# Hybrid decoder block, down projection: GpSimd's additions given to VectorE, the final norm's squares put into another buffer, the last two row blocks normed by halves

## The chip, the core and the metric

The kernel runs on one core of one Trainium2 chip. The metric is the device time of one execution in microseconds (us); a kernel's time is the median of its runs.

## The reference, cut to what matters

The block mixes tokens (an S5 state space branch and an RWKV-7 branch), projects, and ends with a squared-ReLU MLP and a final RMSNorm. Only the last product and the norm are touched here: `hid` has 2048 tokens of 4096 features, `w_down` is 4096 by 1024, `h` is 2048 by 1024, all in float32.

```python
hn = rms_norm(h, norm_ffn_g[i])
h = h + jnp.square(jax.nn.relu(hn @ w_up[i])) @ w_down[i]
return rms_norm(h, norm_final_g)
```

## The kernel before, in words

The program's last stage is `mlp_down`. It computes `hid @ w_down` by a Strassen scheme (Winograd's form): a block of 2 by 2 sub-blocks is multiplied with seven products in place of eight. The products are numbered 1 to 7 and stand in the order 1, 5, 6, 2, 7, 3, 4 (`ORDER`).

The 4096 features are cut into eight groups (`gr`), 512 features each. Within a group eight steps (`c`) go over the tokens; a step adds to two row blocks of 128 tokens, `r0` and `r1`, which stay in SBUF for the whole stage as `acc0` to `acc15` (`r0` of step c is `acc(2c)`, `r1` is `acc(2c+1)`). Their halves of 512 columns are `a11`, `a12` (in `r0`), `a21`, `a22` (in `r1`). So 64 steps of seven products run in all. Below, "4.1:7" is product 7 of step 1 in group 4.

One product is six matmuls of 128x128x512 (`product`, line 1328): both operands are split in a high and a low float32r part (`split`, lines 368 to 378: ScalarE casts the high part, line 374; VectorE subtracts for the low part, line 377), and high by high, high by low, low by high are added up in PSUM. PSUM holds three kinds of tile: `ps_da` (three buffers; products 1, 6, 7, 4 of a step add up in one), `ps_dx` (two; products 5 and 3) and `ps_db` (two; product 2). `ps_da` is read four times in its life. After products 1, 6 and 7 ScalarE copies it to a tile `c` (`later`, line 1624) and the copy is added to a quarter of the rows (line 1620): `c1` and `c3` by GpSimd, `c2` by VectorE. After product 4 VectorE adds the PSUM tile itself. `ps_dx` and `ps_db` are added by VectorE. TensorE can't write the next product into `ps_da` before the copy is done, and can't begin a step whose PSUM buffer has not been read out.

The weights of a group come as two tiles `wraw` (two buffers, 1 MB each, lines 1578 to 1581). `right_sums` makes seven operands of them, with four subtractions in place on VectorE (lines 1309, 1311, 1315, 1318), and each operand is split into `w0h`, `w0l` to `w8h`, `w8l`, so the weights of the next group are made while a group ends and the next begins. The left operands of products 5, 6, 7, 3 come ready and split from DRAM as tiles `hs` (512 KB for two steps, pool `mdh`, tag `hs`, five buffers, line 1594); those of 1, 2, 4 as `hr` (256 KB, line 1598) and are split here into `hh` and `hl`. All these loads, and the output's stores, are issued in order by one queue, SyncE's (SP).

In the last group each row block is normed once its step is done: ScalarE squares the row into a scrap tile `junk` and sums it into `fss` (line 1654), `rms_rows` scales on VectorE (line 385) and takes the power -0.5 on GpSimd (line 386), VectorE multiplies the row in place (line 1656), and SP stores it (line 1657). `junk` is allocated from the same tag as the `hs` tiles. The order of all instructions is set by the Tile framework's scheduler, which also chooses the buffer that a tile gets; an edit can therefore move instructions that it doesn't name.

Of the kernel before, what the change touches and what calls it, by code (L numbers as in the profile page):

```python
# [7 lines left out]
F32 = mybir.dt.float32  # L8
F32R = mybir.dt.float32r
I32 = mybir.dt.int32  # L10
AF = mybir.ActivationFunctionType
ALU = mybir.AluOpType
# [1544 lines left out]
def mlp_down(K, h_dram, hs_dram, hr_dram, w_down, fin_g, out):  # L1557

    nc, tc = K.nc, K.tc
    v, act, g = nc.vector, nc.scalar, nc.gpsimd  # L1560
    NG, NC = 8, NT // 256
    from contextlib import ExitStack
    with ExitStack() as st:
        pool_ = lambda **k: st.enter_context(pool_of(tc, **k))

        hp, wa, kp, fp, rp, op, wb, ap0, ap2 = (pool_(name="md" + n, bufs=1) for n in ("h", "wa", "c", "f", "r", "o", "wb", "a0", "a2"))
        ap1, wc, wd_ = (pool_(name="md" + n, bufs=1, side="right") for n in ("a1", "wc", "wd"))
        psp = pool_(name="mdps", bufs=2, space=PSUM)
        wpool, apool = [wb, wb, wa, wb] + [wc] * 4 + [wd_], [ap0] * 2 + [ap1] * 10 + [ap2] * 4
        dma = g  # L1570
        rows = lambda c: [(c // 4) * 1024 + i * BT + c % 4 * P for i in range(2)]

        def ws():
            n = 0
            for k in range(0, 32, 4):
                wk = w_down[0, k * P:(k + 4) * P, :].rearrange("(a i p) n -> i p a n", i=2, p=P)
                r = [rp.tile([P, 2, 1024], F32, tag="wraw", bufs=2, name="wraw") for _ in range(2)]
                for i in range(2):
                    dma.dma_start(out=r[i], in_=wk[i])
                for o in right_sums(v, [[r[i][:, :, j * 512:j * 512 + 512] for j in range(2)] for i in range(2)]):  # L1580
                    yield halves_of(K, wpool[n % 9], o, [P, 2, 512], f"w{n % 9}", 1)
                    n += 1

        def hs():
            for gr in range(NG):
                for c in range(0, NC, 2):
                    hb, tk, fs, ops = c // 4, slice(c % 4 * P, c % 4 * P + 256), slice(2 * gr, 2 * gr + 2), {}
                    for i in range(2):
                        for n in ORDER:
                            if i:  # L1590
                                pass
                            elif n in SPLIT:
                                t = hp.tile([P, 2, 2, 256], F32R, tag="hs", bufs=5, name="hs")
                                dma.dma_start(out=t.bitcast(F32), in_=hs_dram[hb, SPLIT.index(n), fs, :, :, tk].rearrange("a l p t -> p a l t"))
                                ops[n] = t[:, :, 0], t[:, :, 1]
                            else:
                                t = op.tile([P, 2, 256], F32, tag="hr", bufs=3, name="hr")
                                dma.dma_start(out=t, in_=hr_dram[hb, fs, PLAIN.index(n), :, tk].rearrange("a p t -> p a t"))
                                ops[n] = split(K, op, t, [P, 2, 256], "h", 4)
                            yield tuple([t[:, k, i * P:i * P + P] for k in range(2)] for t in ops[n])  # L1600

        w, hid = Ahead(ws(), DW), Ahead(hs(), DH)
        acc, fin, first = {}, None, None
        with tc.high_priority():
            w.fill()
            hid.fill()
        dma = nc.sync
        for gr in range(NG):
            wd = {}
            for c in range(NC):  # L1610
                if gr == 0:
                  with tc.issue_after(first.ins) if c else ExitStack():
                    for i in range(2):
                        t = 2 * c + i
                        acc[c, i] = apool[t].tile([P, 1024], F32, tag=f"acc{t}", name=f"acc{t}")
                        ld = nc.sync.dma_start(out=acc[c, i], in_=h_dram[rows(c)[i]:rows(c)[i] + P, :])
                  first = first or ld
                r0, r1 = acc[c, 0], acc[c, 1]
                a11, a12, a21, a22 = r0[:, 0:512], r0[:, 512:], r1[:, 0:512], r1[:, 512:]
                add = lambda eng, o, s: eng.tensor_tensor(out=o, in0=o, in1=s, op=ALU.add)  # L1620

                def later(eng, o, ps, name):
                    t = kp.tile([P, 512], F32, tag="c", bufs=3, name=name)
                    act.copy(out=t, in_=ps)  # L1624
                    add(eng, o, t)

                A, X, B = (psp.tile([P, BT], F32, tag=n, bufs=b, name="ps_d" + n) for n, b in (("a", 3), ("x", 2), ("b", 2)))
                for n in ORDER:
                    if n not in wd:
                        wd[n] = w.take()  # L1630
                    ps, start = {1: (A, True), 5: (X, True), 6: (A, False), 2: (B, True), 7: (A, False), 3: (X, False), 4: (A, False)}[n]
                    product(K, ps, hid.take(), wd[n], start)
                    if n == 1:
                        later(g, a11, A, "c1")
                    elif n == 5:
                        add(v, a22, X)
                    elif n == 6:
                        later(v, a12, A, "c2")
                    elif n == 2:
                        add(v, a11, B)  # L1640
                    elif n == 7:
                        later(g, a22, A, "c3")
                    elif n == 3:
                        add(v, a12, X)
                    else:
                        add(v, a21, A)
                if gr == NG - 1:
                    if fin is None:
                        fin = fp.tile([P, 1024], F32, tag="fin", name="fin")
                        nc.sync.dma_start(out=fin, in_=fin_g.rearrange("(o n) -> o n", o=1).broadcast_to([P, 1024]))  # L1650
                    ss = fp.tile([P, 2], F32, tag="fss", bufs=2, name="fss")
                    for i, r in enumerate((r0, r1)):
                        junk = hp.tile([P, 1024], F32, tag="hs", bufs=5, name="junk")
                        act.activation(out=junk, in_=r, func=AF.Square, accum_out=ss[:, i:i + 1])
                        rs = rms_rows(K, fp, ss[:, i:i + 1], 1, 1024, "frs")
                        v.scalar_tensor_tensor(out=r, in0=r, scalar=rs, in1=fin, op0=ALU.mult, op1=ALU.mult)
                        nc.sync.dma_start(out=out[0, rows(c)[i]:rows(c)[i] + P, :], in_=r)


_INS = ["x", "norm_mix_g", "w_in", "lam_re", "lam_im", "log_dt", "b_re", "b_im", "c_re", "c_im", "d_skip", "w_glu", "b_glu",  # L1660
# [80 lines left out]
```

## Time and profile before

| what | us |
|---|---|
| median of 3 runs | 2601.89 |
| lowest and highest run | 2594.81, 2606.95 |
| the profiled execution, its own time | 2604.97 |
| the span of its profile | 2603.2 |
| TensorE busy in the span | 2451.2 (94%) |
| VectorE busy | 1843.4 (71%) |
| ScalarE busy | 1302.0 (50%) |
| GpSimd busy | 858.4 (33%) |

The profile is of one execution; its time is 3.1 us above the median of the runs. The span leaves out 1.8 us around it. `mlp_down` takes roughly the last 680 us: its first matmul stands at 1923.2 us of the span. TensorE's busy time counts overlapping matmuls, so what it leaves idle is read from its waits and not from the share.

### The profile page before, as it was taken

The numbers are of one execution on the slowest core, as the hardware profiler recorded it, in microseconds if no ns is written. First come the engines' busy times: TensorE is split into PE (matmuls) and PEld (weight loads), VectorE is DVE, ScalarE is ACT, GpSimd is POOL, SyncE is SP. The second block draws the span as 40 slices with busy tenths as digits, with TensorE's granted clock in tenths as the row PEclk, the third lists the DMA queues.
The fourth block names the chain that finished last, engine by engine and source line by source line (L and its number), as shares of the span: only waits on it lengthen the run. The fifth ranks groups of instructions, "written<-read, shape, count | busy, mean of one in ns | idle before, by whom it ended". The sixth has DMA issues, their size and how long they took to land.

```text
span 2603.2 us, 38292 instructions
## 1 busy us (share of the span) xinstructions
PE 2451.2 (94%) x13084; PEld 2030.0 (78%) x13084; DVE 1843.4 (71%) x3194; ACT 1302.0 (50%) x2551; POOL 858.4 (33%) x790
## 2 busy tenths in 40 slices
PE   7999979999898898999899999999989999999997
PEld 6887657786898887888688888888867877777775
DVE  7558797579677768666877678877766656665665
ACT  6355545465444446455476667666643323333333
POOL 1058798711222224221122320332212322332323
PEclk9999989999898998999999999999999999999998
DMA  9656737996776646443576566655495555544544
GB/s 287 206 166 177 221 115 231 251 259 176 181 153 156 145 101 199 145 149 115 178 241 216 198 208 220 242 205 198 166 355 195 175 173 164 171 158 154 186 150 166
DMA packets 540980, 491.50 MB, mean 189 GB/s; under 512 B 187281, under 2 KB 442769, under 8 KB 540785
## 3 DMA queue, kind: packets, MB, share of 16 engines
q1 hardware_dynamic: 539072, 483.54, 59.7%
q0 software_dynamic: 992, 3.67, 0.4%
q8 instruction: 104, 1.70, 0.3%
q10 hardware_dynamic: 720, 1.84, 0.2%
q14 instruction: 92, 0.75, 0.1%
HBM read 303.23 MB, written 180.49 MB: 186 GB/s over the span
## 4 chain that ended last, share of the span: by engine, by line
PE 63%; DVE 13%; DMA 10%; issue 5%; POOL 3%; ACT 3%; SPq 2%; POOLq 0%; ACTq 0%; DVEq 0%
PE ps_ua L1328 13%; PE ps_da L1328 9%; PE ps_ux L1328 7%; PE ps_dx L1328 4%; PE ps_ub L1328 3%; PE ps_db L1328 2%; DMA wraw<-in_w_down 2%; PE ps_o L435 2%; PE ps_o L433 2%; PE ps_o L434 2%; PE ps_z L433 1%; PE ps_z L434 1%; PE ps_z L435 1%; DMA hs<-hs_d 1%; PE ps_b L817 1%
## 5 line engine op out<-in xcount | busy, mean ns | idle before, releaser
L1620 POOL TENSOR_TENSOR acc<-acc,c 128x512 f32<-128x512 f32 x128 | 192.6, 1526 | 454.1 <-ACT c L1624 446.8
L1624 ACT COPY c<-ps_da 128x512 f32<-128x512 f32 x192 | 106.3, 588 | 262.6 <-PE ps_da L1328 261.1
L433 PE MATMUL ps_z<-xh,wh 128*128 128x512 f32 x448 | 183.8, 411 | 15.3 <-DVE zr L617 8.7
L435 PE MATMUL ps_z<-xh,wl 128*128 128x512 f32 x448 | 181.1, 405 | 0.0
L434 PE MATMUL ps_z<-xl,wh 128*128 128x512 f32 x448 | 180.3, 402 | 0.0
L1620 DVE TENSOR_TENSOR acc<-acc,ps_dx 128x512 f32<-128x512 f32 x128 | 87.5, 685 | 122.9 <-PE ps_dx L1328 120.7
L1425 DVE TENSOR_TENSOR wl<-wraw,wh 128x512 fp32r<-128x512 f32 x124 | 104.4, 843 | 28.1 <-ACT wh L1424 27.8
L374 ACT CAST hh<-hr 128x512 fp32r<-128x512 f32 x96 | 59.4, 620 | 117.7 <-PE ps_da L1328 90.4
L433 PEld LDWEIGHTS ps_z<-xh,wh 128*128 128x128 f32 x448 | 87.0, 194 | 40.0 <-DVE zr L617 10.5
L609 DVE TENSOR_TENSOR wl<-wr,wh 128x1024 fp32r<-128x1024 f32 x56 | 85.3, 1523 | 37.5 <-ACT wh L608 37.1
L913 POOL TENSOR_TENSOR DT<-dtc,cst 128x128 f32<-128x128 f32 x128 | 55.8, 467 | 158.2 <-PE ps_pq L920 105.9
L1291 POOL TENSOR_TENSOR ws<-wraw 128x512 f32<-128x512 f32 x28 | 41.2, 1471 | 200.6 <-DMA hs_d<-hh 72.6
L433 PE MATMUL ps_o<-woh,ys 128*128 128x512 f32 x256 | 103.0, 403 | 3.4 <-DVE xrow L1225 2.5
L1424 ACT CAST wh<-wraw 128x512 fp32r<-128x512 f32 x124 | 76.2, 617 | 52.9 <-PE ps_ua L1328 34.2
L434 PE MATMUL ps_o<-wol,ys 128*128 128x512 f32 x256 | 102.1, 399 | 0.0
L435 PEld LDWEIGHTS ps_z<-xh,wl 128*128 128x128 f32 x448 | 86.8, 194 | 19.1 <-issue 0.2
L434 PEld LDWEIGHTS ps_z<-xl,wh 128*128 128x128 f32 x448 | 87.0, 194 | 18.6 <-issue 0.9
L435 PE MATMUL ps_o<-woh,ys 128*128 128x512 f32 x256 | 100.7, 396 | 0.0
L1300 POOL TENSOR_TENSOR ws<-wraw,ws 128x512 f32<-128x512 f32 x28 | 41.7, 1489 | 176.0 <-DVE wl L1425 172.6
L1474 DVE TENSOR_TENSOR hh<-hs,hh 128x512 fp32r<-128x512 f32 x96 | 79.6, 829 | 14.2 <-ACT hh L1473 13.2
L1473 ACT CAST hh<-hs 128x512 fp32r<-128x512 f32 x96 | 59.7, 622 | 57.8 <-DVE hs L1490 21.3
L1425 DVE TENSOR_TENSOR wl<-ws,wh 128x512 fp32r<-128x512 f32 x93 | 66.7, 720 | 30.1 <-ACT wh L1424 25.9
(693 smaller groups left out, 8229.2 us busy)
## 6 DMA issues: line engine op xcount, KB each, us to landing
hs_d<-hh SPq DMA_DIRECT2D x256, 256.0 KB
hs<-hs_d SPq DMA_DIRECT2D x126, 512.0 KB
wraw<-in_w_up SPq DMA_DIRECT2D x62, 512.0 KB
wr<-in_w_in SPq DMA_DIRECT2D x56, 512.0 KB
hr<-hr_d SPq DMA_DIRECT2D x94, 256.0 KB
hr_d<-c SPq DMA_DIRECT2D x93, 256.0 KB
xrow<-in_x SPq DMA_DIRECT2D x32, 512.0 KB
wraw<-in_w_down SPq DMA_DIRECT2D x14, 1024.0 KB
```

Of the source, the lines that this page charges most:

```text
L374: nc.scalar.copy(out=hi, in_=raw)
L433: K.nc.tensor.matmul(out, lh, rh, start=i == 0, stop=False)
L434: K.nc.tensor.matmul(out, lh, rl, start=False, stop=False)
L435: K.nc.tensor.matmul(out, ll, rh, start=False, stop=i == n - 1)
L609: v.tensor_tensor(out=wl, in0=wr, in1=wh.bitcast(F32), op=ALU.subtract)
L1328: K.nc.tensor.matmul(ps, a[k], b[k], start=start and k + i == 0, stop=k == n - 1 and i == 2, skip_group_check=True)
L1424: act.copy(out=hi, in_=o)
L1425: v.tensor_tensor(out=lo, in0=o, in1=hi.bitcast(F32), op=ALU.subtract)
L1473: act.copy(out=hi, in_=o)
L1474: v.tensor_tensor(out=lo, in0=o, in1=hi.bitcast(F32), op=ALU.subtract)
L1620: add = lambda eng, o, s: eng.tensor_tensor(out=o, in0=o, in1=s, op=ALU.add)
L1624: act.copy(out=t, in_=ps)
```

## The change

It does three things, all in `mlp_down`. The additions of `c1` and `c3` go from GpSimd to VectorE (two per step, 128 in all). The scrap tile of the final norm's squares comes from the buffers of `wraw` (tag `wraw`, pool `mdr`) and no longer from those of `hs`. And the two row blocks of the last step (c = 7 of the last group) are squared, multiplied and stored in two halves of 512 columns each, with one addition of the two sums of squares; for `r1` the second half is squared first.

```diff
                     if n == 1:
-                        later(g, a11, A, "c1")
+                        later(v, a11, A, "c1")
...
                     elif n == 7:
-                        later(g, a22, A, "c3")
+                        later(v, a22, A, "c3")
...
-                    ss = fp.tile([P, 2], F32, tag="fss", bufs=2, name="fss")
+                    ss = fp.tile([P, 2, 2], F32, tag="fss", bufs=2, name="fss")
+
+                    parts = [slice(h * 512, h * 512 + 512) for h in range(2)] if c == NC - 1 else [slice(0, 1024)]
                     for i, r in enumerate((r0, r1)):
-                        junk = hp.tile([P, 1024], F32, tag="hs", bufs=5, name="junk")
-                        act.activation(out=junk, in_=r, func=AF.Square, accum_out=ss[:, i:i + 1])
-                        rs = rms_rows(K, fp, ss[:, i:i + 1], 1, 1024, "frs")
-                        v.scalar_tensor_tensor(out=r, in0=r, scalar=rs, in1=fin, op0=ALU.mult, op1=ALU.mult)
-                        nc.sync.dma_start(out=out[0, rows(c)[i]:rows(c)[i] + P, :], in_=r)
+                        junk = rp.tile([P, 2, 1024], F32, tag="wraw", bufs=2, name="junk")
+                        for h, hs_ in list(enumerate(parts))[::1 - 2 * i]:
+                            act.activation(out=junk[:, 0, hs_], in_=r[:, hs_], func=AF.Square, accum_out=ss[:, i, h:h + 1])
+                        if len(parts) > 1:
+                            v.tensor_tensor(out=ss[:, i, 0:1], in0=ss[:, i, 0:1], in1=ss[:, i, 1:2], op=ALU.add)
+                        rs = rms_rows(K, fp, ss[:, i, 0:1], 1, 1024, "frs")
+                        for hs_ in parts:
+                            v.scalar_tensor_tensor(out=r[:, hs_], in0=r[:, hs_], scalar=rs, in1=fin[:, hs_], op0=ALU.mult, op1=ALU.mult)
+                            nc.sync.dma_start(out=out[0, rows(c)[i]:rows(c)[i] + P, hs_], in_=r[:, hs_])
```

The scheduler moves other instructions too. Three places matter for the prediction.

VectorE where group 3 passes into group 4 (`acc13` and `acc14` belong to steps 6 and 7 of group 3, `acc1` to step 0 of group 4; `w8l` is a weight of a later group). Before:

```order
L1620 TENSOR_TENSOR acc12_20060<-acc12_20060,ps_dx_21881 128x512
L377 TENSOR_TENSOR w8l_22110<-wraw_22105,w8h_22109 128x1024
L1309 TENSOR_TENSOR wraw_22105<-wraw_22105 128x2x512
L1620 TENSOR_TENSOR acc1_19587<-acc1_19587,ps_dx_22023 128x512
L1620 TENSOR_TENSOR acc14_20138<-acc14_20138,ps_db_21956 128x512
L1620 TENSOR_TENSOR acc13_20062<-acc13_20062,ps_da_21880 128x512
```

Now:

```order
L1620 TENSOR_TENSOR acc12_20060<-acc12_20060,ps_dx_21881 128x512
L1620 TENSOR_TENSOR acc13_20062<-acc13_20062,c3_21937 128x512
L1620 TENSOR_TENSOR acc14_20138<-acc14_20138,c1_21963 128x512
L1620 TENSOR_TENSOR acc14_20138<-acc14_20138,ps_db_21956 128x512
L377 TENSOR_TENSOR w8l_22110<-wraw_22105,w8h_22109 128x1024
L1620 TENSOR_TENSOR acc13_20062<-acc13_20062,ps_da_21880 128x512
L1309 TENSOR_TENSOR wraw_22105<-wraw_22105 128x2x512
```

The two additions of `c` are new on VectorE, and the addition that frees `ps_db` of step 3.7 now stands ahead of the two weight instructions, where it stood behind them.

ScalarE at the same place. Before:

```order
L1624 COPY c2_21915<-ps_da_21880 128x512
L374 CAST w8h_22109<-wraw_22105 128x1024
L1624 COPY c3_21937<-ps_da_21880 128x512
L1624 COPY c1_21963<-ps_da_21954 128x512
L1624 COPY c2_21979<-ps_da_21954 128x512
```

Now:

```order
L1624 COPY c2_21915<-ps_da_21880 128x512
L1624 COPY c3_21937<-ps_da_21880 128x512
L1624 COPY c1_21963<-ps_da_21954 128x512
L374 CAST w8h_22109<-wraw_22105 128x1024
L1624 COPY c2_21979<-ps_da_21954 128x512
```

The cast `w8h`, which has to wait for a load of `wraw`, no longer stands ahead of the copies of 3.6:7 and 3.7:1.

SP's queue in the last group, from the store of `acc4` on (`hs_24221` and `hs_24230` are the left operands of products 7 and 3 of steps 4 and 5, `hs_24342`, `hs_24351`, `hs_24393` and `hs_24402` those of 5, 6, 7 and 3 of steps 6 and 7). Before:

```order
L1657 DMA out_0<-acc4_19760 128x1024 [waits DMAHW3_49,DVE_49]
L1657 DMA out_0<-acc5_19762 128x1024 [waits DMAHW4_49,DVE_49]
L1657 DMA out_0<-acc6_19838 128x1024 [waits DMAHW5_49,DVE_49]
L1594 DMA hs_24221<-hs_d_75 128x4x256 [waits PE_49]
L1594 DMA hs_24230<-hs_d_75 128x4x256 [waits DMAHW7_49,Activation_49]
L1657 DMA out_0<-acc7_19840 128x1024 [waits DMAHW0_49,DVE_49]
L1594 DMA hs_24342<-hs_d_75 128x4x256 [waits DMAHW7_49,DMAHW1_49,PE_49]
L1594 DMA hs_24351<-hs_d_75 128x4x256 [waits DMAHW2_49,Activation_49]
L1657 DMA out_0<-acc8_19910 128x1024 [waits DMAHW3_49,DVE_49]
L1657 DMA out_0<-acc9_19912 128x1024 [waits DMAHW4_49,DVE_49]
L1657 DMA out_0<-acc10_19988 128x1024 [waits DMAHW5_49,DVE_49]
L1594 DMA hs_24393<-hs_d_75 128x4x256 [waits DMAHW6_49,PE_49]
```

Now:

```order
L1663 DMA out_0<-acc4_19760 128x1024 [waits DMAHW4_49,DVE_49]
L1594 DMA hs_24230<-hs_d_75 128x4x256 [waits DMAHW5_49,PE_49]
L1594 DMA hs_24342<-hs_d_75 128x4x256 [waits DMAHW6_49,PE_49]
L1663 DMA out_0<-acc5_19762 128x1024 [waits DMAHW7_49,DVE_49]
L1594 DMA hs_24351<-hs_d_75 128x4x256 [waits DMAHW0_49,PE_49]
L1663 DMA out_0<-acc6_19838 128x1024 [waits DMAHW1_49,DVE_49]
L1594 DMA hs_24393<-hs_d_75 128x4x256 [waits DMAHW5_49,DMAHW2_49,PE_49]
L1663 DMA out_0<-acc7_19840 128x1024 [waits DMAHW3_49,DVE_49]
L1663 DMA out_0<-acc8_19910 128x1024 [waits DMAHW4_49,DVE_49]
L1594 DMA hs_24402<-hs_d_75 128x4x256 [waits PE_49]
```

No load waits for ScalarE (the squares) any more, and a load has fewer stores of unfinished rows ahead of it: `hs_24393` stood behind the store of `acc10`, now it stands behind that of `acc6`.

## Rows read from the trace of the kernel before

**Rows 1.** Page, part 4: the chain of work that ended last.

```profile
PE 63%; DVE 13%; DMA 10%; issue 5%; POOL 3%; ACT 3%; SPq 2%; POOLq 0%; ACTq 0%; DVEq 0%
```

**Rows 2.** Waits of TensorE, 1975 to 2500 us: total us, times, longest.

```profile
PE ps_db L1328 <- DVE acc L1620: 10.8, 6, 1.8
PE ps_da L1328 <- DVE acc L1620: 4.1, 5, 2.5
PE ps_da L1328 <- ACT c L1624: 1.3, 5, 0.3
```

**Rows 3.** Timeline of TensorE, groups 3 to 4: start, us; idle before.

```profile
2260.39 0.50 PE L1328 MATMUL ps_db<-w4h,hh 128*128 128x512 f32 x1 [1.81 <-DVE acc L1620]
...
2280.79 0.51 PE L1328 MATMUL ps_da<-w1h,hh 128*128 128x512 f32 x1 [0.70 <-DVE acc L1620]
```

**Rows 4.** Timeline of VectorE at the same place.

```profile
2255.03 1.23 DVE L377 TENSOR_TENSOR w8l<-wraw,w8h 128x1024 fp32r<-128x1024 f32 x1 [3.15 <-ACT w8h L374]
2256.29 2.20 DVE L1309 TENSOR_TENSOR wraw<-wraw 128x1024 f32<-128x1024 f32 x1
...
2259.65 0.69 DVE L1620 TENSOR_TENSOR acc<-acc,ps_db 128x512 f32<-128x512 f32 x1 [0.56 <-POOL acc L1620]
```

**Rows 5.** Timeline of GpSimd: a pair of additions at the boundary, another later.

```profile
2255.56 4.06 POOL L1620 TENSOR_TENSOR acc<-acc,c 128x512 f32<-128x512 f32 x2 [7.88 <-ACT c L1624]
...
2305.43 2.54 POOL L1620 TENSOR_TENSOR acc<-acc,c 128x512 f32<-128x512 f32 x2 [5.76 <-ACT c L1624]
```

**Rows 6.** Lines 1309 and 1318 on VectorE: ns least/median/most.

```profile
L1309 DVE TENSOR_TENSOR wraw<-wraw x8: 1225/2194/2201, 1924.5 to 2420.5; 128x1024 f32<-128x1024 f32 x8
L1318 DVE TENSOR_TENSOR wraw<-wraw x8: 1209/1218/1219, 1935.9 to 2487.7; 128x1024 f32<-128x1024 f32 x8
```

**Rows 7.** Windows: us, busy of PE, PEld, DVE, ACT, POOL (count), clock, DMA, GB/s.

```profile
2008.00:2018.00 10.00, 8.17 (x29) 6.30 (x28) 6.29 (x10) 4.53 (x7) 2.48 (x2) 0.83 0.23 69
...
2580.00:2590.00 10.00, 8.50 (x30) 6.61 (x30) 3.74 (x6) 2.68 (x5) 3.10 (x3) 0.83 0.35 127
```

**Rows 8.** Windows of a boundary of groups and of the 40 us behind it.

```profile
2244.00:2284.00 40.00, 37.25 (x159) 29.14 (x158) 31.23 (x35) 13.86 (x21) 14.29 (x8) 1.00 0.57 191
2284.00:2324.00 40.00, 40.00 (x175) 32.44 (x174) 18.62 (x28) 12.26 (x21) 10.20 (x8) 1.00 0.45 146
```

**Rows 9.** Line 1620: additions of copies on GpSimd and VectorE.

```profile
L1620 POOL TENSOR_TENSOR acc<-acc,c x121: 1273/1296/2292, 1973.8 to 2593.6; 128x512 f32<-128x512 f32 x121
...
L1620 DVE TENSOR_TENSOR acc<-acc,c x60: 675/692/694, 1979.2 to 2591.2; 128x512 f32<-128x512 f32 x60
```

**Rows 10.** Load of the weights: issue on SP, and VectorE's wait.

```profile
2269.24 0.37 SPq L1579 DMA_DIRECT2D wraw<-in_w_down  x1
```

**Rows 11.** VectorE behind that load.

```profile
2276.08 1.23 DVE L1311 TENSOR_TENSOR wraw<-wraw 128x1024 f32<-128x1024 f32 x1 [2.61 <-DMA wraw<-in_w_down]
```

**Rows 12.** Waits of TensorE, 2500 us to the end.

```profile
PE ps_da L1328 <- DMA hs<-hs_d: 7.5, 3, 3.6
PE ps_da L1328 <- ACT c L1624: 2.6, 3, 1.1
```

**Rows 13.** SP's queue in the last group.

```profile
2554.46 0.33 SPq L1657 DMA_DIRECT2D out<-acc  x1
2554.85 1.37 SPq L1594 DMA_DIRECT2D hs<-hs_d  x2
```

**Rows 14.** Timeline of TensorE in the last group.

```profile
2559.51 0.47 PE L1328 MATMUL ps_da<-w8h,hs 128*128 128x512 f32 x1 [2.02 <-DMA hs<-hs_d]
...
2591.22 0.50 PE L1328 MATMUL ps_da<-w8h,hs 128*128 128x512 f32 x1 [1.11 <-ACT c L1624]
```

**Rows 15.** Timelines of ScalarE, VectorE and SP at the end.

```profile
2596.08 1.06 ACT L1654 ACTIVATE junk<-acc 128x1024 f32<-128x1024 f32 x1 [1.21 <-DVE acc L1620]
...
2598.17 1.28 DVE L1656 SCALAR_TENSOR_TENSOR acc<-acc,frs,fin 128x1024 f32<-128x1024 f32 x1 [0.73 <-POOL frs L386]
...
2599.49 0.33 SPq L1657 DMA_DIRECT2D out<-acc  x1
```

## The prediction, made before the change was run

> **What bounds the kernel now.** I read the chain of work that ended last first: TensorE carries 63% of it [rows 1], so a change in the down projection is worth what it takes out of TensorE's waits there, and no more. The next view is therefore TensorE's waits. From 1975 to 2500 us, where one group of features passes into the next seven times or is about to, it waits 10.8 us for additions into the rows that free `ps_db`, 4.1 us for such additions that free `ps_da`, and 1.3 us for copies: 16.2 us in 16 waits [rows 2]. From 2500 us on it waits 7.5 us in three waits for `hs` loads and 2.6 us in three waits for copies [rows 12]. The timeline puts the first kind at the boundaries of groups, where weights are made: in the boundary of groups 3 and 4 the waits are 1.81 and 0.70 us [rows 3].
>
> VectorE's timeline says why. The subtraction of line 1309 took 2.20 us, and the addition that frees `ps_db` came behind it and then waited 0.56 us more for GpSimd [rows 4]. Line 1309 takes 1.23 us at its quickest, and line 1318 never takes more than 1.22 [rows 6]; they are of one size. What differs is GpSimd: it was adding two copies from 2255.56 to 2259.62, and those took 4.06 us, where a pair takes 2.54 with VectorE not reading two SBUF tiles beside it [rows 5]. So the two engines slow each other, and the instruction that began second loses: `w8l`, begun 0.53 us before GpSimd's additions, kept its 1.23 us [rows 4].
>
> The third view is the granted clock. Around seven of the longer waits (four at boundaries, three for `hs`) it is 0.83 over 10 us (the first and the last of the seven windows are shown), part of the stretch at 1.2 GHz and the rest at 2.4 [rows 7]: 1.7 us lost each time, behind an idle TensorE. The boundary with waits of 1.81 and 0.70 us kept 1.00 [rows 8], so not every wait is followed by it.
>
> **The change, part by part.** The sum is made against the profiled execution, 2605.0 us, which is 3.1 above the median of the runs.
>
> *Additions.* VectorE takes over two additions a step, 128 in all. One of GpSimd's takes 1.30 us at the median, VectorE's of the same shape 0.69 [rows 9]. Over a step of 9.6 us (42 matmuls at 40.0/175 = 0.229 us [rows 8]) that is 1.4 us. Away from boundaries VectorE is busy 18.6 of 40 us [rows 8]; four steps' worth, 5.5 us, leaves it at 24, which TensorE covers. At a boundary it is busy 31.2 of 40 us [rows 8]; it gets the same 5.5 us and gets rid of what GpSimd cost it. I count five instructions there that were slowed by 0.5 to 1.1 us; at line 1309's 0.97 (2.20 less 1.23) they make 4.8. So about 32 of 40 us: no saturation, and additions that no longer wait for GpSimd.
>
> The Trainium skill ("SBUF — State Buffer", Who interferes with whom) says that a VectorE instruction with two SBUF inputs and a GpSimd instruction that reads SBUF exclude each other, and that the one that starts second is blocked until the first ends. The trace agrees on who loses, with 0.97 us on line 1309 and nothing on `w8l`. By that rule a collision may cost up to a whole addition of GpSimd, 1.27 us, so five would give back 6.4 in place of 4.8, and the sum below would end some 2 us lower.
>
> Now the order. At the boundary 3 to 4 the two copies no longer stand behind the cast `w8h`, and the addition that frees `ps_db` stands ahead of `w8l` and of line 1309. VectorE can have done it by about 2254, before TensorE comes to ask at 2258.6 (2260.39 less 1.81 [rows 3]). That wait goes. The second one depends on a load. Line 1311 waits for weights until 2276.08 [rows 11]; the load was issued at 2269.24 [rows 10], 6.8 us before, behind `w7l`, which also ran beside GpSimd. Now `w7l` stands ahead of the addition of `ps_dx` and is unslowed: TensorE ends 3.7:7 at about 2261.8, two copies take ScalarE to 2263.1, the cast to 2264.2, and `w7l` ends at 2265.6, so the load lands at 2272.4. Then come two subtractions (1.2 each) and five additions (0.6 each, as they overlap a little): 2277.8. TensorE, without its earlier waits, asks for that buffer at 2277.0. So 0.3 to 0.9 us stays; I take 0.5 at each of seven boundaries, 3.5 in all. Bounds: nothing stays, or the load comes no earlier and everything stays. Gain: 16.2 + 4 x 1.7 - 3.5 = **19.5 us**, between 0 and 23.0.
>
> *The squares' buffer.* The `hs` loads of the last group waited for buffers that `junk` held and stood in SP's queue behind stores of rows not yet normed: two loads followed the store of `acc6` by 0.4 us [rows 13], and the product that needed the first began at 2559.51, 4.7 us after its issue, having waited 2.02 [rows 14]. Now a load waits for TensorE alone and stands behind stores of earlier rows. I walked all eight loads of steps 2 to 7 that follow a store: each is issued four products or more (5.5 us) ahead of its use, except the one for 7.2:3, which has three products (4.1 us) against 4.5 to 4.7: 0.5 us. Another 0.4 us may come at 7.7:1, where the addition that frees `ps_da` stands behind a norm's scaling. Of the short waits for copies one goes (7.0:4 no longer follows 7.0:7) and one comes (7.6:4 now follows 7.6:7). `wraw`'s buffers are free by then: the last load into them is of the last group's weights. Gain: 7.5 + 3 x 1.7 - 0.9 = **11.7 us**, between 0 (queue still late) and 12.6.
>
> *Halves at the end.* The last square takes 1.06 us, the last scaling 1.28, and the last store is issued at 2599.49 [rows 15], 3.7 us before the span ends. Half a square saves about 0.5 us; the addition of two sums costs about 0.15; the second half's store is issued no earlier, but is half as large: between 0 and 1.9 us, I take 0.7, below the middle, as no row shows a store of half the size. Against that, the copy `c3` of 7.7 now stands on ScalarE behind both squares of `acc14`, so TensorE's wait there and the one of 1.11 us before it [rows 14] grow, by some 1 us together. Sum: **0**, between -2 and +1.5.
>
> Together 31.2 us: 2605.0 - 31.2 = **2574 us**. From the median it would be 2571; I keep 2574, as small waits are easily missed in such a walk.
>
> **The rivals.** *VectorE inherits the boundary waits.* Additions that GpSimd did on its own now queue behind weight subtractions, and VectorE waits in order for a load (2.61 us [rows 11]) with two additions behind it. If all 23 us stay, only the loads gain: 2605.0 - 11.7 = 2593 us, no change that counts. For it: VectorE is the busiest engine there after TensorE. Against: the walk. The Trainium skill ("Perfetto Trace Analysis", Optimizing Scalar/DVE Operations) says that work may go to GpSimd where VectorE is saturated, but that it may not help, as the two share a read port; the first half speaks against this change, and 31.2 of 40 us says that VectorE is close to it at boundaries only.
>
> *The loads stay late.* If the norms' stores, which now wait for a busier VectorE, hold the queue as before, only the boundaries gain: 2605.0 - 19.5 = 2585 us, still faster by 0.6%.
>
> *No relief.* If line 1309 is slow for another reason than GpSimd, VectorE has 5.5 us more at each boundary and gets nothing back. About 1.5 us a boundary would be added to waits (10 us) and the loads would still gain: about 2603. Against: line 1318 and `w8l`.
>
> *Slower.* A step in the even stretches has only about 0.8 us between VectorE's freeing of `ps_db` and TensorE's need of it, because `c1`'s addition now stands in front in the same queue. If each step's additions come later than my walk by more than that, TensorE waits in 56 steps; at 1.8 us late it is 56 x 1.0 - 31 = 25 us slower, 2630. It decides from 1.4 us on. Against: VectorE idle in half of those stretches [rows 8].
>
> **How the numbers follow.** A measurement can tell about 0.5% here, 13 us. Forecast 0.65; inherited waits 0.13; loads late 0.11; no relief 0.06; slower 0.05. Faster: forecast and late loads, with a little of the first rival's near edge, 0.77; same 0.18; slower 0.05. The range reaches from 2564 (all 35.6 us and the end's 2 us, from the median) to 2594 (only the loads gain), and leaves out the last two rivals and the far tails.
>
> **What would show it.** Right: no GpSimd addition on line 1620; lines 1309 and 1315 at 1.2 us throughout; TensorE's waits for additions at boundaries down from 14.9 us to some 4; no wait for `hs` above 1 us in the last group; granted clock near 1.00 to within 10 us of the end. Wrong: TensorE waiting for line 1620 as long as before, or on products 2 and 1 in every step; stores of rows just ahead of a load that TensorE waits for; lines 1309 and 1315 still at 2.2.

## Result, and the profile after

The changed kernel takes 2567.1 us at the median of 4 runs (2562.7 to 2568.0), the kernel before 2599.6 beside it (2594.8 to 2607.0): a ratio of 0.987, 95% interval 0.9854 to 0.9886. The prediction of 2574 us, faster, holds. Of the 7 us by which the forecast lies above the median, 5.4 are its starting point, a profiled execution of 2605.0 us, where the runs beside the changed kernel have a median of 2599.6; the gain itself was forecast at 31.2 us and is 32.5. The profiled execution took 2566.7 us, its span is 2565.0 us against 2603.2.

Medians of one kernel differ by a few us from chip to chip, and the span holds 1900 us that the change doesn't touch (line 1309 first runs at 1918.9 us now, at 1924.5 before [rows 6], with the same instructions ahead of it; so 5.6 of the 38.2 us between the two profiles were not gained by the change). So I measure the stage by three marks on TensorE, in the view of a tile's instructions (first and last start stand at the end of a row). After:

```profile
L1309 DVE TENSOR_TENSOR wraw<-wraw x8: 1218/1220/1225, 1918.9 to 2395.7; 128x1024 f32<-128x1024 f32 x8
...
L1328 PE MATMUL ps_da<-w1h,hs x64: 388/396/403, 2326.5 to 2480.0; 128*128 128x512 f32 x64
...
L1328 PE MATMUL ps_da<-w1h,hl x32: 387/393/398, 2234.4 to 2556.4; 128*128 128x512 f32 x32
```

and before:

```profile
L1328 PE MATMUL ps_da<-w1h,hs x64: 388/395/403, 2351.9 to 2506.5; 128*128 128x512 f32 x64
...
L1328 PE MATMUL ps_da<-w1h,hl x32: 387/394/398, 2252.8 to 2594.9; 128*128 128x512 f32 x32
```

The last `ps_da<-w1h,hs` is product 6.7:7, behind the last boundary of groups; the last `ps_da<-w1h,hl` is TensorE's last matmul. **Groups** is from the first start of line 1309 to 6.7:7, **last group** from there to the last matmul, **tail** from there to the end of the span.

| us | before | after | gain | predicted |
|---|---|---|---|---|
| groups | 582.0 | 561.1 | 20.9 | 19.5 |
| last group | 88.4 | 76.4 | 12.0 | 11.7 less 1 for two copies |
| tail | 8.3 | 8.6 | -0.3 | about 1 |
| whole stage | 678.7 | 646.1 | 32.6 | 31.2 |

TensorE's waits after, from 1960 to 2500 us (these answer to [rows 2]) and from 2500 us on ([rows 12]):

```profile
PE ps_db L1328 <- DVE acc L1620: 5.0, 6, 1.0
```

```profile
PE ps_da L1328 <- ACT c L1624: 2.8, 3, 1.1
PE ps_da L1328 <- DVE acc L1620: 0.3, 1, 0.3
```

Sixteen waits of 16.2 us have become six of 5.0, one at each of six boundaries of groups (the prediction reckoned with seven); the waits for `hs` in the last group are gone. On VectorE the subtractions that took 2.2 us take 1.2, all of them, and the additions of copies are as quick as the few that it had before ([rows 6, 9] answer to these; the first row below is line 1315 before, the others are after):

```profile
L1315 DVE TENSOR_TENSOR wraw<-wraw x8: 1218/2313/2320, 1927.9 to 2440.3; 128x1024 f32<-128x1024 f32 x8
...
L1315 DVE TENSOR_TENSOR wraw<-wraw x8: 1217/1218/1225, 1922.4 to 2414.0; 128x1024 f32<-128x1024 f32 x8
...
L1620 DVE TENSOR_TENSOR acc<-acc,c x192: 680/689/695, 1923.6 to 2555.2; 128x512 f32<-128x512 f32 x192
```

Windows of the changed kernel: the groups, the last group up to 2555 us, the boundary of groups 3 and 4 and the 40 us behind it (the last two answer to [rows 8]; columns as there):

```profile
1975.00:2485.00 510.00, 504.97 (x2174) 407.47 (x2173) 361.99 (x512) 179.31 (x280) 0.00 (x0) 1.00 0.52 171
2485.00:2555.00 70.00, 67.00 (x287) 53.11 (x285) 54.97 (x86) 32.31 (x62) 9.30 (x14) 1.00 0.55 194
```

```profile
2220.00:2260.00 40.00, 39.28 (x171) 31.70 (x170) 33.68 (x45) 17.67 (x26) 0.00 (x0) 1.00 0.60 197
2260.00:2300.00 40.00, 40.00 (x174) 32.44 (x174) 22.59 (x36) 10.36 (x18) 0.00 (x0) 1.00 0.44 145
```

GpSimd is idle through the groups. The granted clock is 1.00 in both stretches: none of the seven losses of [rows 7] is left. VectorE is busy 33.7 of 40 us at the boundary (predicted: about 32) and 22.6 behind it (predicted: 24).

The boundary of groups 3 and 4, where the prediction was walked through, on VectorE:

```profile
2246.34 1.22 DVE L377 TENSOR_TENSOR w7l<-wraw,w7h 128x1024 fp32r<-128x1024 f32 x1
...
2254.90 1.23 DVE L1311 TENSOR_TENSOR wraw<-wraw 128x1024 f32<-128x1024 f32 x1 [3.04 <-DMA wraw<-in_w_down]
2256.04 1.22 DVE L1315 TENSOR_TENSOR wraw<-wraw 128x1024 f32<-128x1024 f32 x1
2257.18 1.29 DVE L1620 TENSOR_TENSOR acc<-acc,c 128x512 f32<-128x512 f32 x2
2258.38 0.68 DVE L1620 TENSOR_TENSOR acc<-acc,ps_dx 128x512 f32<-128x512 f32 x1
2258.97 0.69 DVE L1620 TENSOR_TENSOR acc<-acc,ps_db 128x512 f32<-128x512 f32 x1
```

and on SP and TensorE:

```profile
2247.59 0.37 SPq L1579 DMA_DIRECT2D wraw<-in_w_down  x1
```

```profile
2259.72 0.50 PE L1328 MATMUL ps_db<-w4h,hh 128*128 128x512 f32 x1 [0.72 <-DVE acc L1620]
```

`w7l` ends, the load is issued at once and lands 7.3 us later; VectorE stands idle before line 1311 for the last 3.04 us with two subtractions and the additions behind it; the fourth of these frees `ps_db`, and TensorE, which came 0.72 us too early, goes on. That is the chain of the prediction, with 0.5 us forecast at its end.

### The profile page after: what moved, and what is told of

Its sections match the earlier page's. It is cut to its first block, busy times and chain, and to the rows that moved or that the text cites. A ratio compares the mean times of both kernels' runs of the same rounds, so it can differ in the third digit from the quotient of the medians.

```text
span 2565.0 us, 38224 instructions
## 1 busy us (share of the span) xinstructions
PE 2434.8 (95%) x13084; PEld 2020.9 (79%) x13084; DVE 1886.5 (74%) x3326; ACT 1301.6 (51%) x2555; POOL 667.4 (26%) x662
## 4 chain that ended last, share of the span: by engine, by line
PE 70%; DVE 12%; DMA 9%; ACT 3%; issue 2%; POOL 2%; SPq 1%; DVEq 0%; POOLq 0%; ACTq 0%
PE ps_ua L1328 13%; PE ps_da L1328 11%; PE ps_ux L1328 7%; PE ps_dx L1328 5%; PE ps_ub L1328 3%; PE ps_db L1328 3%; PE ps_o L433 2%; PE ps_o L435 2%; PE ps_o L434 2%; DMA wraw<-in_w_down 2%; PE ps_z L433 1%; PE ps_z L434 1%; PE ps_z L435 1%; DMA wr<-in_w_in 1%; DVE acc L1620 1%
## 5 line engine op out<-in xcount | busy, mean ns | idle before, releaser
L1620 DVE TENSOR_TENSOR acc<-acc,c 128x512 f32<-128x512 f32 x192 | 127.3, 689 | 105.0 <-ACT c L1624 104.8
L386 POOL TENSOR_TENSOR frs<-frs,mhalf 128x1 f32<-128x1 f32 x16 | 10.4, 650 | 645.0 <-DVE frs L385 645.0
L1424 ACT CAST wh<-wraw 128x512 fp32r<-128x512 f32 x124 | 76.1, 616 | 52.8 <-PE ps_ua L1328 34.1
```

The source lines that it names most:

```text
L1424: act.copy(out=hi, in_=o)
```

## The experiments

Each kernel is the kernel before or the changed kernel with one edit. All lengths are of one profiled execution each; the marks are those above.

| kernel | median us (runs) | ratio to before, 95% interval | groups | last group | tail |
|---|---|---|---|---|---|
| changed, first | 2567.1 (4) | 0.9870, 0.9854 to 0.9886 | 561.1 | 76.4 | 8.6 |
| additions alone | 2581.1 (6) | 0.9909, 0.9890 to 0.9928 | 559.1 | 85.2 | 9.5 |
| buffer alone | 2592.4 (7) | 0.9951, 0.9932 to 0.9969 | 581.2 | 75.8 | 8.3 |
| halves alone | 2603.1 (12) | 0.9997, 0.9980 to 1.0014 | 584.6 | 89.3 | 7.9 |
| changed, no halves | 2571.9 (5) | 0.9875, 0.9854 to 0.9896 | 560.1 | 76.8 | 8.9 |
| scrap additions | 2604.1 (12) | 1.0006, 0.9991 to 1.0021 | 597.3 | 76.4 | 8.6 |
| `c3` on GpSimd | 2579.1 (6) | 0.9914, 0.9893 to 0.9936 | 573.7 | 81.4 | 8.7 |
| loads split | 2570.6 (6) | 0.9879, 0.9860 to 0.9899 | 562.0 | 76.4 | 8.7 |
| end reordered | 2569.2 (4) | 0.9872, 0.9850 to 0.9894 | 559.6 | 76.1 | 7.8 |
| later loads split | 2565.8 (4) | 0.9862, 0.9839 to 0.9885 | 557.2 | 76.3 | 8.7 |
| split and end | 2566.2 (4) | 0.9868, 0.9850 to 0.9887 | 556.2 | 76.0 | 8.0 |
| changed, again | 2570.3 (4) | 0.9883, 0.9866 to 0.9900 | 562.8 | 76.3 | 8.6 |

The kernel before stood at 2604.4 us beside the four runs after the first row, at 2602.0 beside the next four, at 2601.1 beside the last three.

### The three parts one by one

Additions alone (kernel before, with this edit):

```diff
-                        later(g, a11, A, "c1")
+                        later(v, a11, A, "c1")
...
-                        later(g, a22, A, "c3")
+                        later(v, a22, A, "c3")
```

> The kernel before with c1's and c3's additions on VectorE and nothing else changed. My theory (the boundaries pay 16.2 us of waits and 6.8 us of clock because GpSimd's additions slow VectorE and stand in front of the addition that frees ps_db): 18 us faster than before, about 2581 us, TensorE's waits for additions between 1975 and 2485 us at about 5 us, the three waits for hs loads of about 2 to 3.6 us each still there. Rival (the parts only work together, because the scheduler's order of the loads decides): under 8 us faster, with boundary waits above 12 us.

Buffer alone:

```diff
-                        junk = hp.tile([P, 1024], F32, tag="hs", bufs=5, name="junk")
+                        junk = rp.tile([P, 2, 1024], F32, tag="wraw", bufs=2, name="junk")[:, 0]
```

> The kernel before with the squares' scrap tile in the weights' buffers and nothing else changed. My theory: the three waits for hs loads in the last group (7.5 us and 5.1 us of clock) go or stay under 1 us each, the boundary waits stay at about 16 us; 11 to 12 us faster than before, about 2588 us. Rival (the stores of unfinished rows in the queue hold the loads, whoever owns the buffer): two or more waits for hs of 1.5 us and more remain, under 5 us faster.

Halves alone: the kernel before with the changed kernel's `parts`, `junk` still from the buffers of `hs`.

> The kernel before with the last two row blocks squared, scaled and stored by halves and nothing else changed. My theory after the changed kernel's trace: the last store is half as large and ends about 0.7 us sooner after its issue, but the scaling of acc14 in two halves stands in front of the last addition on VectorE; from the last matmul's end to the end of the span about 8 us as before; the time the same within 2 us. Rival (halves are worth what they were made for): 1.5 us or more less from the last matmul to the end.

The changed kernel without halves:

```diff
-                    parts = ... if c == NC - 1 else [slice(0, 1024)]
+                    parts = ... if c == NC else [slice(0, 1024)]
```

> The changed kernel without the halves (additions and buffer only). TensorE's order is the changed kernel's. My theory: the end of the span comes at the same time to within 1 us, since the halves gain about 0.7 us at the store and lose about as much in VectorE's order; 2567 us. Rival (the halves cost what the last group lost in my sum): 1.5 us faster than the changed kernel, or the halves help: 1.5 us slower.

TensorE's waits, for additions alone from 1975 to 2485 us, and all that there are for the buffer alone from 2500 us on:

```profile
PE ps_db L1328 <- DVE acc L1620: 2.6, 4, 1.0
```

```profile
PE ps_da L1328 <- ACT c L1624: 2.6, 3, 1.1
```

The parts act where the prediction put them. The additions shorten the groups by 22.9 us (582.0 to 559.1) and, unforeseen, the last group by 3.2, where one of the three waits for `hs` went as well (5.9 us in two are left), while the tail grows by 1.2; the buffer shortens the last group by 12.6 and the groups by 0.8, which is within what one kernel's traces differ by (561.1 and 562.8 for the changed one). The halves do nothing that the times can show: 0.9997 alone, and 0.9875 against 0.9870 without and with them. By the marks they are worth 0.7 us in the changed kernel (76.8 + 8.9 against 76.4 + 8.6). By medians the first two parts give 23.3 and 12.0 us (expected: 18, and 11 to 12), 35 together, where the whole change gives 32.5; their intervals are some 5 us wide on either side, so this difference says nothing. How much of the buffer's gain comes from the buffer itself and how much from the shorter queue of stores ahead of the loads was not separated, as the one edit changes both.

### Is it the second engine, or the room on VectorE?

The prediction said that VectorE gains because GpSimd no longer collides with it. The rival: GpSimd's additions were merely slow or late. So VectorE keeps all additions, and GpSimd gets its old work back as scrap that no one waits for, in groups 0 to 6; it adds into `fin`, which is loaded only at step 0 of the last group:

```diff
+        g.memset(fin[:, 0:512], 0.0)
...
                     add(eng, o, t)
+                    if name != "c2" and gr < NG - 1:
+                        add(g, fin[:, 0:512], t)
```

> The changed kernel, with GpSimd adding c1 and c3 of the first seven groups into a scrap tile that nobody reads (extra work, 112 additions of 128x512 in SBUF). No addition into the rows waits for GpSimd, so only the contention of the two engines is put back. My theory (contention is a good part of the boundary waits): lines 1309 and 1315 at about 2.2 us again, TensorE's boundary waits up from 5 us to 8 to 14 us, 4 to 12 us slower than the changed kernel. Rival (the boundary waits came from the addition that frees ps_db waiting for GpSimd's addition into the same row, and the slow subtractions were covered): boundary waits stay at 5 to 6 us and the time within 2 us of the changed kernel, though lines 1309 and 1315 are slow.

It costs the whole gain, far more than I expected: 32 to 35 us by the ratios (1.0006 against 0.9883 and 0.9870). In its profile the groups are 36 us longer than the changed kernel's and 15 longer than those of the kernel before; that execution, 2611.9 us, is 7.8 above its median, so these two lengths are at the high end. VectorE's instructions by line and form from 1975 to 2495 us (count | busy us, mean ns of one | idle before):

```profile
L1621 DVE TENSOR_TENSOR acc<-acc,c 128x512 f32<-128x512 f32 x147 | 162.9, 1135 | 73.1 <-ACT c L1625 73.1
L1621 DVE TENSOR_TENSOR acc<-acc,ps_dx 128x512 f32<-128x512 f32 x100 | 68.1, 681 | 1.5
...
L1315 DVE TENSOR_TENSOR wraw<-wraw 128x1024 f32<-128x1024 f32 x6 | 12.8, 2130 | 0.0
```

and the first group of these by least, median and most ns:

```profile
L1621 DVE TENSOR_TENSOR acc<-acc,c x147: 677/694/1796, 1979.5 to 2492.0; 128x512 f32<-128x512 f32 x147
```

Additions with both operands in SBUF take 1135 ns on the mean in place of 689: half of them are not slowed (median 694), the slowest takes 1796. Line 1315 takes 2130 on the mean in place of 1218; line 1309, which I had expected to be slow as well, keeps 1218. Additions with one operand in PSUM keep 681. Nothing in this trace waits for a scrap addition, so the copies' tiles, which GpSimd now reads too, are not what holds the kernel up. TensorE pays twice. At the boundaries its waits grow (the row is for 1960 us on) and the clock falls with them: four 20 us windows stand at 0.91, as the first of the two below, and two neighbours at 0.95 and 0.97. And in between it now stops where it did not: in the second window the clock is 1.00, but TensorE is idle 0.15 us, and 86 matmuls stand where the changed kernel has 88 in 20 us.

```profile
PE ps_db L1328 <- DVE acc L1621: 22.8, 21, 4.0
```

```profile
2120.00:2140.00 20.00, 18.18 (x72) 14.64 (x73) 11.55 (x17) 4.46 (x8) 3.56 (x3) 0.91 0.46 145
2060.00:2080.00 20.00, 19.85 (x86) 15.79 (x85) 13.17 (x19) 5.18 (x9) 6.72 (x4) 1.00 0.48 147
```

The second of the two is what the prediction's rival "slower" described: an even step leaves VectorE little slack, and the collisions take it. How the 36 us divide between boundaries and steps I did not settle. Nor does any run give VectorE's instructions the scheduler's old order without the collisions, so how much of the 20.9 us in the groups is due to the new order (the addition that frees `ps_db` now stands ahead of two weight instructions) and how much to the end of the collisions stays open. What is shown is that GpSimd's work beside VectorE is enough to take the gain away; it meets more here than in the kernel before, as VectorE now has all three additions of a step's copies in place of one.

### One of the two additions back on GpSimd

```diff
-                        later(v, a22, A, "c3")
+                        later(g, a22, A, "c3")
```

> The changed kernel with c3's additions back on GpSimd: c1, whose row's next addition frees ps_db, stays on VectorE, so no addition of VectorE that frees a buffer waits for GpSimd, and GpSimd does half of its additions of before. My theory: some of lines 1309, 1311 and 1315 slow (2.2 us), boundary waits between 5 and 10 us, 1 to 6 us slower than the changed kernel. Rival (the dependence alone): the same as the changed kernel or 1 to 3 us faster, as VectorE has 64 additions less.

8 to 11 us slower than the changed kernel by the ratios (0.9914 against 0.9883 and 0.9870), again more than expected. Its profiled execution, 2591 us, is 12 us above its median, so its lengths are at the high end; its mechanism is plain all the same. TensorE's waits for the addition that frees `ps_db` are back, from 1960 to 2500 us:

```profile
PE ps_db L1328 <- DVE acc L1620: 10.7, 6, 1.9
```

GpSimd's timeline and VectorE's at two places:

```profile
2066.79 1.29 POOL L1620 TENSOR_TENSOR acc<-acc,c 128x512 f32<-128x512 f32 x1 [9.83 <-ACT c L1624]
...
2075.12 2.07 POOL L1620 TENSOR_TENSOR acc<-acc,c 128x512 f32<-128x512 f32 x1 [7.04 <-ACT c L1624]
```

```profile
2067.24 1.39 DVE L1620 TENSOR_TENSOR acc<-acc,c 128x512 f32<-128x512 f32 x1 [4.60 <-ACT c L1624]
2068.55 0.68 DVE L1620 TENSOR_TENSOR acc<-acc,ps_dx 128x512 f32<-128x512 f32 x1
...
2074.82 1.22 DVE L377 TENSOR_TENSOR w7l<-wraw,w7h 128x1024 fp32r<-128x1024 f32 x1
2075.96 1.79 DVE L1620 TENSOR_TENSOR acc<-acc,c 128x512 f32<-128x512 f32 x1
2077.67 0.68 DVE L1620 TENSOR_TENSOR acc<-acc,ps_dx 128x512 f32<-128x512 f32 x1
```

First place: GpSimd runs until 2068.08; VectorE's addition, begun inside it, gives way to the next 0.47 us later, most of its own length. Second place: `w7l` began first and keeps 1.22 us; GpSimd, begun inside it, needs 2.07; VectorE's next addition waits for GpSimd's end at 2077.19 and needs 1.79. So the second does not run slower, it waits until the first is done. The Trainium skill ("SBUF — State Buffer", Who interferes with whom) has just this: a VectorE instruction with two SBUF inputs and a GpSimd instruction that reads SBUF lock each other out, whoever comes first keeping the port, and a VectorE instruction with at most one SBUF input, outside its two-port modes, goes free. These rows agree with the lock, and the 681 ns of the additions from PSUM above with the exception.

### What is left at the boundaries

The remaining 0.7 to 1.0 us a boundary should come from VectorE standing before line 1311 for a 1 MB load. So the load comes in halves of 512 columns, in order of need:

```diff
-                    dma.dma_start(out=r[i], in_=wk[i])
+                    for j in ((0, 1), (1, 0))[i]:
+                        dma.dma_start(out=r[i][:, :, j * 512:j * 512 + 512], in_=wk[i][:, :, j * 512:j * 512 + 512])
```

> The changed kernel with each load of the weights issued as two halves of 512 KB, in the order in which the subtractions need them. In the changed kernel VectorE waits 19.2 us in six boundaries for line 1311's load, with the additions that free ps_db queued behind it, and TensorE waits 5.0 us there. My theory (that load is what is late next): VectorE's wait there falls by 1 us or more a boundary and TensorE's boundary waits fall under 2 us; 3 to 5 us faster than the changed kernel. Rival (more loads in the queue or the contention of transfers cost as much, or the next thing late is the copies): the same, boundary waits 4 us or more.

No gain, but not because the reason was wrong. VectorE's idle time before line 1311 fell from 19.2 to 2.8 us (1975 to 2500 us, changed kernel and this one: total, times, longest), and no boundary has a wait for `ps_db` left.

```profile
DVE wraw L1311 <- DMA wraw<-in_w_down: 19.2, 6, 3.4
```

```profile
DVE wraw L1311 <- DMA wraw<-in_w_down: 2.8, 6, 1.0
```

It was given back at the start of the stage. TensorE's waits from 1900 to 1960 us, those that are new:

```profile
PE ps_db L1328 <- ACT w3h L374: 4.3, 1, 4.3
PE ps_db L1328 <- DVE w3l L377: 1.3, 1, 1.3
```

In group 0 nothing covers the loads, and with the halves the operand `w3` is ready later than TensorE asks for it. So the next kernel splits the loads of groups 1 to 7 only:

```diff
-                    dma.dma_start(out=r[i], in_=wk[i])
+                    for j in ((slice(0, 512), slice(512, 1024)), (slice(512, 1024), slice(0, 512)))[i] if k else (slice(0, 1024),):
+                        dma.dma_start(out=r[i][:, :, j], in_=wk[i][:, :, j])
```

> The changed kernel with the weights' loads of groups 1 to 7 in two halves of 512 KB in order of need, those of group 0 whole. Theory: what is left at the six boundaries of the groups (5.0 us of waits for the addition of ps_db in the changed kernel's trace) comes from VectorE standing before line 1311 until a whole 1 MB load has landed (19.2 us idle there in six times), and splitting all groups took that away (0.4 us of such waits, 2.8 us idle) but gave it back in group 0, where TensorE waited 4.3 us for w3h and 1.3 us for w3l. So with group 0 whole: ps_db waits under 1 us, no wait for w3h at the start, the stretch from the first sum of line 1309 to the end of the span 641 to 642 us against 646.1, and the median 4 to 5 us under the changed kernel's. Rival (more, smaller transfers slow the queue itself, or VectorE is late for another reason next): the boundary waits go and other waits take their place, stretch 645 to 648 us, median as the changed kernel's within 2 us.

The stage takes 642.2 us, 0.2 above what was expected (647.7 for the changed kernel run beside it), and the median is 4.6 us below that kernel's. All of TensorE's waits from 1960 to 2500 us:

```profile
PE ps_dx L1328 <- DVE acc L1621: 0.4, 1, 0.4
```

### The end

The last addition from PSUM stood behind the scaling of `acc14`, and a copy behind its second square (rows in the next section). The edit puts the scaling behind that addition (`da`) and the square behind the copy (`c3`); `end` is true in the last step of the last group:

```diff
-                            act.activation(out=junk[:, 0, hs_], ...)
+                            with tc.issue_after(c3.ins) if end and i == 0 and h else ExitStack():
+                                act.activation(out=junk[:, 0, hs_], ...)
...
-                            v.scalar_tensor_tensor(out=r[:, hs_], ...)
+                            with tc.issue_after(da.ins) if end and i == 0 else ExitStack():
+                                v.scalar_tensor_tensor(out=r[:, hs_], ...)
```

> The changed kernel with two instructions of the last step issued later: the scaling of acc14 behind the last addition into acc15, and the square of acc14's second half behind the last copy c3. In the changed kernel the last addition began 1.3 us after the last matmul's end, and the last matmuls waited 1.02 us for c3. My theory (VectorE and ScalarE keep program order, so these two places cost the halves their gain): the last addition begins at once, the wait for c3 falls to about 0.7, and the span from the start of 7.7:6 to the end is 1.3 to 1.8 us shorter. Rival (the stores of acc14 then pile up in front of acc15's): under 0.5 us shorter.

The tail went from 8.6 to 7.8 us and the last copy's wait from 1.02 to 0.67. From the start of 7.7:6 to the end of the span it is 1.1 us less (15.2 to 14.1), short of the 1.3 to 1.8 expected; the median can't show it. VectorE now waits for the last product instead of coming 1.2 us late:

```profile
2563.31 0.69 DVE L1620 TENSOR_TENSOR acc<-acc,ps_da 128x512 f32<-128x512 f32 x1 [0.42 <-PE ps_da L1328]
```

Both edits together, the split of the later loads and this one:

> The kernel of the run before with the end reordered as in the earlier run (the scaling of the last row block but one behind the last addition, its second square behind the last copy). That reordering brought the end from the last product to the end of the span from 8.2 to 7.4 us and cut the last copy's wait from 1.02 to 0.67 us. Theory: both are independent: stretch from the first sum of line 1309 to the end of the span 640 to 641 us, median 5 to 6 us under the changed kernel's. Rival: if the end hides behind the last store's landing, no difference to the run before (under 0.5 us in the stretch).

The stage takes 640.2 us, the shortest of all, 7.5 below the changed kernel run beside it. Of the 2.0 us below the split alone, 1.0 lies in the groups, which the second edit doesn't touch; from 7.7:6 to the end it is again 1.1 us (15.3 to 14.2). The median is 4.2 below the changed kernel's, where 5 to 6 were expected, and not distinguishable from the split alone.

The changed kernel once more, with no edit:

> The changed kernel once more, on the chip of the two runs before, as their measure: by the theory its ps_db waits at the six boundaries sum to 2.6 to 5.0 us again (they hang on when each load lands, which differs between runs: 2.6, 3.9 and 5.0 us in three traces with the same additions), the clock stays at 1.00 from 1975 us until the last product, and its median is 33 us under the kernel before (ratio 0.987). If the gain of the first measurement were of that chip or run, the ratio would lie above 0.990.

0.9883, and five waits for `ps_db` of 4.5 us in sum: the gain is not one of chip or run. The two versions with split loads are the best here, but the intervals of their ratios overlap with this one's, so it is the traces, not the times, that show them ahead.

## Why the prediction was right

**The bound and the place.** TensorE's waits at boundaries and for `hs` were the money, as read from [rows 2, 12]. Groups and last group gained 20.9 and 12.0 us, and each part alone acts mainly on its own stretch.

**Additions, 19.5 us forecast, 20.9 measured.** Two terms were off, in opposite directions. What stays at boundaries was put at 3.5 us; it is 5.0 in this trace, and 2.6, 3.9, 3.2 and 4.5 in four others with the same additions (alone; no halves; end reordered; again), as it hangs on when a load lands. The mean of the five is 3.8, so the term was good and the single trace was not. The term that was mis-sized is the price of a wait: the sum counted the idle time that the view lists, and a stop costs more. TensorE's timeline after, around one:

```profile
2100.36 0.40 PE L1328 MATMUL ps_da<-w7l,hs 128*128 128x512 f32 x1
2100.59 0.39 PE L1328 MATMUL ps_da<-w7h,hs 128*128 128x512 f32 x1
2101.97 0.50 PE L1328 MATMUL ps_db<-w8h,hh 128*128 128x512 f32 x1 [0.99 <-DVE acc L1620]
2102.31 0.40 PE L1328 MATMUL ps_db<-w8l,hh 128*128 128x512 f32 x1
```

Matmuls follow each other by 0.23 us; here the gap is 1.38, and the next one 0.34: 1.26 us lost for 0.99 listed, 0.27 more. Of these, 0.16 is how the view counts: it lets the idle time begin where the last matmul ends, 0.39 us after its start, though the next would have started 0.23 us after it. The other 0.11 is the longer gap behind the first matmul. The stop of 1.81 us in [rows 3] comes to 0.27 more as well (matmuls start at 2258.19, 2260.39 and 2260.73 us). Ten stops fewer make 2.7 us. Then 16.2 - 5.0 + 2.7 + 4 x 1.7 for the clock = 20.7, against 20.9. For the prediction's "instruction that began second loses" the runs put a lock in place of a slowdown, and line 1315, at 2.31 us before and 1.22 now, lost 1.10 us where I reckoned with 0.97.

**The squares' buffer, 11.7 us forecast, 12.0 measured.** No wait for `hs` remained in the last group; the two waits of 0.4 to 0.5 us that the walk left (7.2:3, 7.7:1) came as one of 0.28, for an addition. By the rows: waits from 10.1 us in six to 3.1 in four, 7.0; two stops fewer, 0.5; the clock, 5.1: 12.6. `7.6:4` got its wait (0.73), `7.0:4` lost it, as said.

**The end, 0 forecast.** Halves gained 0.7 us by the marks, but the tail as a whole lost 0.3 where I had counted on some 1 us. TensorE's waits for the last copies, VectorE and ScalarE at the end of the changed kernel:

```profile
2552.45 0.50 PE L1328 MATMUL ps_da<-w8h,hs 128*128 128x512 f32 x1 [1.10 <-ACT c L1624]
...
2555.13 0.50 PE L1328 MATMUL ps_da<-w1h,hh 128*128 128x512 f32 x1 [1.02 <-ACT c L1624]
```

```profile
2556.67 1.42 DVE L1662 SCALAR_TENSOR_TENSOR acc<-acc,frs,fin 128x512 f32<-128x512 f32 x2 [0.73 <-POOL frs L386]
2558.00 0.68 DVE L1620 TENSOR_TENSOR acc<-acc,ps_da 128x512 f32<-128x512 f32 x1
```

```profile
2553.88 0.63 ACT L1657 ACTIVATE junk<-acc 128x512 f32<-128x512 f32 x1 [0.86 <-DVE acc L1620]
2554.42 0.19 ACT L1657 ACTIVATION_READ_ACCUMULATOR junk<-acc 128x1 f32 x1
2554.51 0.57 ACT L1624 COPY c<-ps_da 128x512 f32<-128x512 f32 x1
```

The copies' two waits were 1.11 and 0.73 us before and are 1.10 and 1.02: they grew by 0.28, not by 1. What I missed is on VectorE: the scaling of `acc14`, two halves of 1.42 us together, stands in its queue ahead of the last addition. TensorE's last matmul ends at 2556.8; the addition starts at 2558.00. Moving it shortened the tail by 0.8 us.

**The rivals.** VectorE did not inherit the boundary waits; it is idle 19.2 us before line 1311 in six times (14.2 before), and what it inherited is the 5.0 us. The `hs` loads of the last group are not late. "No relief" is refuted by lines 1309 and 1315. "Slower" did not come: from 1960 to 2500 us TensorE waits only at six boundaries. With the scrap additions, where VectorE's additions collide again, it waits in the even stretches too, and the groups come out longer than in the kernel before.

## What to carry to other kernels

Work given to GpSimd to relieve VectorE is paid for by every VectorE instruction with two SBUF inputs that meets it: before moving work there, count those that stand on the path of the bounding engine, and prefer that VectorE read PSUM while GpSimd works. A buffer that a late consumer borrows from a prefetch's ring turns that consumer's queue into the prefetch's queue. When an idle engine waits in order for a big load with urgent small work behind it, split the load in order of need, but only where other work covers its start (here the traces show this gain, the times do not tell it from noise).

## What the hardware showed that was not expected

A stop of TensorE cost 0.27 us more than the idle time listed for it. And GpSimd work that nobody waits for, 112 additions of 1.6 us at the median, cost 32 to 35 us on the path: VectorE's 147 additions with two SBUF inputs grew by 446 ns on the mean, 66 us in all, though half of them not at all, while 100 additions from PSUM kept their 681 ns.
